# Masks on ScalarE, fixed convolution inputs, and weights split by casting and accumulating transfers in a two-block transformer kernel

## The chip, the cores and the metric

The kernel runs on one core of one Trainium2 chip. The metric is the time of one execution on the device in microseconds. The kernel before took 1448.87 us, the median of three runs (1448.43 to 1448.95).

The engines go by their names in the profile: PE is TensorE (matmuls; PEld is its loading of the stationary operand), DVE is VectorE, ACT is ScalarE, POOL is GpSimd, and SP is the queue that issues most transfers.

## The reference

Two different blocks act one after the other on 512 tokens of width 1024, all in float32. Biases, masks and gains are left out here.

```python
# first block
hn = rmsnorm(h, norm_mix_w)
q, k, v, z, xbc, dt_raw = split(hn @ w_in)
att = chunk_band_attention(q, k, v, rel_bias)          # 8 heads of 64
xbc = silu(causal_depthwise_conv(xbc, conv_w, conv_b))  # 4 taps, 1536 channels
y = ssd_scan(x, dt, A, Bm, Cm) + d_skip * x             # 16 heads, 2 groups, state 128
ssd = gated_group_norm(y * silu(z))
h = h + concat([att, ssd]) @ w_out
h = h + square(relu(rmsnorm(h) @ w_ff1)) @ w_ff2        # 4096 hidden
h = rmsnorm(h)
# second block
z = rmsnorm(x) @ w_in_2                                 # pooled part, q, k, v
y_pool = pool_mixer(u_pool);  y_attn = diff_attention(q, k, v)
gates = sigmoid(h @ w_gate + b_gate)
x = x + (gates_0 * (y_pool @ w_branch_pool) + gates_1 * (y_attn @ w_branch_attn)) @ w_out_2
x = x + square(relu(rmsnorm(x) @ w_up)) @ w_down
```

In the scan, the decay between two positions of a chunk is the exponential of a difference of running sums of `dt * A`.

## The kernel before, in words

**Three matmuls for one.** TensorE multiplies in a reduced float32 format (`F32R`). So that the result is accurate, every operand is split into a high part, which is the value rounded to that format, and a low part, which is the value less its high part. A product is then three matmuls: high by high, high by low and low by high (`mm3` and `mm3s`, lines 167 to 175).

**The weight stream.** Most weights lie in device memory as 172 units of 128 x 1024 float32 (512 KB), in the order of use. `load_unit` (L132) brings the next unit to a raw tile `wr` (pool `wraw`, three buffers) by SP's queue. `ahead` (L144) runs at the first use of each unit: it loads up to three units ahead of the use and splits up to two ahead. The split is a ScalarE copy into a tile `wh` (L156, pool `whi`, two buffers) and a subtraction into a tile `wl` (L157, pool `wlo`, two buffers), on VectorE, or on POOL for units 1 and 3 only. Both are marked with high priority. `st["lim"]` holds the splitting back, not the loading.

**Order of the work.** TensorE's instructions keep the order in which the program writes them. `drive` advances one dense product and, between its steps, a step of the side jobs (convolution, scan, attention). For the other engines a planner orders the instructions by priority and by its own estimate of when they are ready; each engine's queue then works strictly in that order. A tile of a pool takes a buffer that has been released by all its readers.

**First stage.** `dense1` (L789) projects the convolution's channels first: four blocks of B and C by `quad`, then eight of x by `rows`. Each block ends in `conv` (L475). It takes an input tile `u` of 515 columns (two buffers), clears its first three columns on POOL (L477), scales the product into the rest (L478), and forms four taps (L480 on ScalarE, L482 on VectorE), a tanh and a product (L485, L486). `xs_side` (L544) then transposes the blocks on TensorE (L548).

**Masks.** `dt_side` makes `da`, split into `dah` and `dal`, for 4 chunks x 16 heads. For the scan, `am_pair` (L560) multiplies a 128 x 128 triangle (`le`) by four of these columns at once, on POOL: 128 x 512 for the high part (L563), and the same for the low part (L565). There are 16 pairs: two for each of four chunks and two groups. A pair is the moving operand of L599 and L600.

**Feed-forward.** It runs in two blocks, `a` and `b`, each in four quarters. A quarter first makes 1024 hidden channels with 8 units of the stream (`hidden`), then `second` (L943) multiplies them by a part of the second matrix, with a scheme of seven products for eight (sums and differences of halves). The second matrix does not pass through the unit stream: `load2` (L888) brings 128 x 1024 tiles `u` and `v`, and `prep` (L910) forms their differences and splits them. A half-width operand goes through `narrow` (L893; tiles `vh` and `vl`). A full-width one goes through `wide` (L898), which takes its tiles **from the pools `whi` and `wlo`** of the unit stream and splits by L298 on ScalarE and L299 on VectorE. `second` walks through stages 0, 1 and 2 with four steps each; stages 0 and 1 have one wide operand in each step, stage 2 none. A step prepares operands up to two steps ahead. The first two are prepared in the hidden stage, ahead of the use of its last unit. In the last step of a stage, the products are done in the reverse order:

```python
            for r, key in enumerate(seq):
                for m in seq[r:r + 3]:
                    prep(m)
                if r == len(seq) - 2:
                    st["lim"] = N_UNITS
                    ahead()
                ...
                for t in (reversed(todo) if e else todo):
                    prod(*t)
```

**Second block.** Its attention (`a2_first` to `a2_third`) keeps POOL in use: squares (L1172), scalings (L1178, L1275), the second map's weight (L1252), and `stack_q`'s low part (L358).

Of the kernel before, what the change touches and what calls it, by code (L numbers as in the profile page):

```python
# [9 lines left out]
F32 = mybir.dt.float32  # L10
F32R = mybir.dt.float32r
I32 = mybir.dt.int32
AF = mybir.ActivationFunctionType
ALU = mybir.AluOpType
# [4 lines left out]
T = 512  # L19
# [6 lines left out]
N_UNITS = 172  # L26
# [22 lines left out]
def bc_mid(ap, n):  # L49
    return ap.rearrange("p (o a) -> p o a", o=1).to_broadcast([ap.shape[0], n, ap.shape[1]])  # L50


def bc_in(ap, n):
    return ap.rearrange("p (a o) -> p a o", o=1).to_broadcast([ap.shape[0], ap.shape[1], n])
# [36 lines left out]
def mixer_kernel(ctx, tc, xT, xN, wst, wfa, wfb, wdt, wgrp, rbt, par, con, frow, out):  # L91
    nc = tc.nc
    V, S, G, PE = nc.vector, nc.scalar, nc.gpsimd, nc.tensor

    const = ctx.enter_context(tc.tile_pool(name="const", bufs=1))
    base = ctx.enter_context(tc.tile_pool(name="base", bufs=1))
    wraw_p = ctx.enter_context(tc.tile_pool(name="wraw", bufs=3))
    whi_p = ctx.enter_context(tc.tile_pool(name="whi", bufs=2))
    wlo_p = ctx.enter_context(tc.tile_pool(name="wlo", bufs=2))
    sm = ctx.enter_context(tc.tile_pool(name="sm", bufs=3))  # L100
    ps_mm = ctx.enter_context(tc.tile_pool(name="ps_mm", bufs=4, space=PSUM))
    ps_ax = ctx.enter_context(tc.tile_pool(name="ps_ax", bufs=4, space=PSUM))
# [16 lines left out]
    def C(name):  # L119
        a, b = _CON[name]  # L120
        return con_sb[:, a:b]
# [2 lines left out]
    wdt_sb = const.tile([128, KD, 16], F32, name="wdt")  # L124

    st = {"raw": {}, "dma": 0, "hl": {}, "split": 0, "use": 0, "pool": 2, "tick": 0, "lim": N_UNITS}
    RAW_AHEAD, SPLIT_AHEAD = 3, 2

    def parts(j):
        return [slice(0, 512), slice(512, 1024)] if j == 0 else [slice(0, 1024)]  # L130

    def load_unit(between=None):  # L132
        j = st["dma"]
        if j < N_UNITS:
            t = wraw_p.tile([128, 1024], F32, tag="wr", name="wr")
            for p in parts(j):
                nc.sync.dma_start(out=t[:, p], in_=wst[j][:, p])
                if between:
                    between()
                    between = None  # L140
            st["raw"][j] = t
            st["dma"] += 1

    def ahead():  # L144
        u = st["use"]
        with tc.high_priority():
            while st["dma"] < min(u + RAW_AHEAD, N_UNITS):
                load_unit()
            while st["split"] < min(u + SPLIT_AHEAD, st["lim"]):
                j = st["split"]  # L150
                t = st["raw"].pop(j)
                hi = whi_p.tile([128, 1024], F32R, tag="wh", name="wh")
                lo = wlo_p.tile([128, 1024], F32R, tag="wl", name="wl")
                eng = G if st["pool"] and j % st["pool"] == 1 else V
                for p in parts(j):
                    S.activation(out=hi[:, p], in_=t[:, p], func=AF.Copy)  # L156
                    eng.tensor_tensor(out=lo[:, p], in0=t[:, p], in1=hi.bitcast(F32)[:, p], op=ALU.subtract)  # L157
                st["hl"][j] = (hi, lo)
                st["split"] += 1

# [16 lines left out]
    def col(w, j):  # L177
        return w[:, j * 128:(j + 1) * 128]
# [122 lines left out]
    def v3(ap, a=NT):  # L301
        return ap.rearrange("p (a b) -> p a b", a=a)
# [100 lines left out]
    with ExitStack() as ph:  # L403
        fa_p = ph.enter_context(tc.tile_pool(name="m1f", bufs=1))
        s_p = ph.enter_context(tc.tile_pool(name="m1s", bufs=2))
        c_p = ph.enter_context(tc.tile_pool(name="m1c", bufs=1))
# [40 lines left out]
        def small(name, n=64):  # L447
            return c_p.tile([128, n], F32, name=name)

        dx, du, dz, dz2, dp, dt, da, dal = (  # L450
            small(n) for n in ("dx", "du", "dz", "dz2", "dp", "dt", "da", "dal"))
        dah = c_p.tile([128, 64], F32R, name="dah")
        aexp = small("aexp", 16)
        ex = small("ex", 192)
        dtdo = small("dtdo")

        xs_tok, conv_out, lw = {}, {}, {}
        ready = set()

# [13 lines left out]
            yield True  # L473

        def conv(f, b):  # L475
            u = s_p.tile([128, T + 3], F32, tag="u", name="u", bufs=2)
            G.memset(u[:, 0:3], 0.0)  # L477
            V.tensor_tensor(out=u[:, 3:], in0=b, in1=lw["rb1"], op=ALU.mult)  # L478
            a = FA.get()
            S.activation(out=a, in_=u[:, 3:], func=AF.Identity, bias=cb_[:, f:f + 1], scale=cw[:, 36 + f:37 + f])  # L480
            for j in range(3):
                V.scalar_tensor_tensor(out=a, in0=u[:, j:j + T], scalar=cw[:, j * 12 + f:j * 12 + f + 1], in1=a,  # L482
                                       op0=ALU.mult, op1=ALU.add)
            t = FA.get()
            S.activation(out=t, in_=a, func=AF.Tanh)  # L485
            V.scalar_tensor_tensor(out=a, in0=t, scalar=1.0, in1=a, op0=ALU.add, op1=ALU.mult)  # L486
            FA.put(t)
            conv_out[f] = a
            ready.add(("conv", f))
# [70 lines left out]
        def am_pair(c, g, q):  # L560
            o = c * 16 + g * 8 + q * 4
            amh, aml = RA.take(2)
            G.tensor_tensor(out=v3(amh), in0=bc_mid(C("le"), 4), in1=bc_in(dah.bitcast(F32)[:, o:o + 4], 128),  # L563
                            op=ALU.mult)
            G.tensor_tensor(out=v3(aml), in0=bc_mid(C("le"), 4), in1=bc_in(dal[:, o:o + 4], 128), op=ALU.mult)  # L565
            return amh, aml

        def ssd_side():
# [472 lines left out]
    with ExitStack() as ph:  # L1041
# [39 lines left out]
        us = {}  # L1081
# [415 lines left out]
```

## Time and profile before

| | |
|---|---|
| median of three runs | 1448.87 us |
| the profiled execution | 1448.68 us |
| its span | 1446.9 us |
| TensorE busy | 1423.2 us (98%) |
| VectorE busy | 1019.4 us (70%) |
| ScalarE busy | 660.8 us (46%) |
| POOL busy | 276.8 us (19%) |
| L157 (low parts of units) | 171 instructions, 231.8 us |
| L156 (high parts of units) | 173 instructions, 182.5 us |
| moved by transfers | 145.90 MB |

A line of a group gives the source line, the engine, the operation, the tile written and the tiles read, the shape and the count; then busy time and the mean of one instruction in ns, and the idle time of that engine just before these instructions, with what ended it. A line of the timeline gives start and length in us; what stands in brackets at its end is idle time before it and what ended it. A line of waits gives the total in us, the number of waits and the longest. A line of a stretch of time gives its length, the busy time of PE, PEld, DVE, ACT and POOL with counts, the granted clock of TensorE as a share, the busy share of the 16 transfer engines, and GB/s. A line of transfers gives what is moved, the issuing queue, the count, the size, and the median us from issue to landing.

### The profile page before, as it was taken

The page shows a single profiled execution, that of the slowest core. Times are in us where ns is not written, and L with a number is a line of the kernel's source. Part 1 is how long each engine was busy: PE and PEld are TensorE (multiplying, and loading weights), DVE is VectorE, ACT ScalarE, POOL GpSimd, SP SyncE. Part 2 cuts the span into 40 slices and gives each one's busy share as a digit, 9 for nine tenths or more (in the row PEclk, how much of TensorE's full clock was granted, in tenths as well). Part 3 has the DMA queues.
Part 4 walks back from the last instruction along what each step waited for, and adds up shares of the span by engine and source line. Part 5 has one row for each costly group of instructions (what it writes and reads, how often), then busy time and mean ns, then how long its engine had stood idle before and what let it go on. Part 6 is the DMA issues. An engine that isn't in the chain of part 4 may idle for free.

```text
span 1446.9 us, 17960 instructions
## 1 busy us (share of the span) xinstructions
PE 1423.2 (98%) x6683; PEld 1172.2 (81%) x6683; DVE 1019.4 (70%) x1761; ACT 660.8 (46%) x1108; POOL 276.8 (19%) x264
## 2 busy tenths in 40 slices
PE   8979999999999999999999999999999999999998
PEld 6857888888888888888878888888888888888887
DVE  7885665655977768677784666777645977878676
ACT  5433445433644435355444646464324544444452
POOL 4664730000010010102262433221110010010101
PEclk9999999999999999999999999999999999999999
DMA  7212532223433241520333433341233433141401
GB/s 255 83 50 65 139 98 82 69 88 116 175 97 114 65 149 44 160 74 30 94 92 95 124 95 100 101 122 62 88 102 133 158 114 105 58 146 45 160 30 58
DMA packets 46407, 145.90 MB, mean 101 GB/s; under 512 B 5872, under 2 KB 6128, under 8 KB 46320
## 3 DMA queue, kind: packets, MB, share of 16 engines
q1 hardware_dynamic: 46320, 144.76, 32.1%
q8 instruction: 52, 0.85, 0.2%
q14 instruction: 35, 0.29, 0.1%
HBM read 131.63 MB, written 2.10 MB: 92 GB/s over the span
## 4 chain that ended last, share of the span: by engine, by line
PE 82%; DVE 9%; POOL 3%; issue 3%; DMA 1%; ACT 1%; SPq 0%; POOLq 0%; DVEq 0%; ACTq 0%
PE mm L168 12%; PE mm L170 12%; PE mm L169 12%; PE mm L173 10%; PE mm L174 10%; PE mm L175 10%; DVE wl L157 2%; PE ax L175 2%; PE ax L173 2%; PE ax L174 2%; DVE s L1253 1%; PE ax L723 1%; PE ax L1265 1%; PE ax L382 1%; PE ax L617 1%
## 5 line engine op out<-in xcount | busy, mean ns | idle before, releaser
L168 PE MATMUL mm<-r,wh 128*128 128x512 f32 x928 | 368.5, 397 | 0.0
L170 PE MATMUL mm<-r,wl 128*128 128x512 f32 x928 | 362.1, 390 | 1.1 <-DVE wl L157 1.1
L169 PE MATMUL mm<-r,wh 128*128 128x512 f32 x928 | 362.0, 390 | 0.9 <-DVE r L294 0.9
L156 ACT ACTIVATE wh<-wr 128x1024 fp32r<-128x1024 f32 (+1 forms) x173 | 182.5, 1055 | 379.4 <-PE mm L169 147.1
L157 DVE TENSOR_TENSOR wl<-wr,wh 128x1024 fp32r<-128x1024 f32 (+1 forms) x171 | 231.8, 1355 | 111.7 <-ACT wh L156 111.1
L173 PE MATMUL mm<-wh,r 128*128 128x512 f32 x512 | 206.0, 402 | 0.0
L169 PEld LDWEIGHTS mm<-r,wh 128*128 128x128 f32 x928 | 174.7, 188 | 38.4 <-issue 1.4
L170 PEld LDWEIGHTS mm<-r,wl 128*128 128x128 f32 x928 | 174.5, 188 | 38.4 <-DVE wl L157 1.5
L168 PEld LDWEIGHTS mm<-r,wh 128*128 128x128 f32 x928 | 174.8, 188 | 37.3 <-issue 1.9
L175 PE MATMUL mm<-wh,r 128*128 128x512 f32 x512 | 200.0, 391 | 0.0
L174 PE MATMUL mm<-wl,r 128*128 128x512 f32 x512 | 199.5, 390 | 0.3 <-DVE wl L157 0.3
L299 POOL TENSOR_TENSOR vl<-u,vh 128x512 fp32r<-128x512 f32 x36 | 47.8, 1330 | 754.9 <-ACT vh L298 754.5
L174 PEld LDWEIGHTS mm<-wl,r 128*128 128x128 f32 x512 | 96.3, 188 | 21.5 <-issue 1.9
L173 PEld LDWEIGHTS mm<-wh,r 128*128 128x128 f32 x512 | 96.2, 188 | 20.8 <-issue 1.9
L175 PEld LDWEIGHTS mm<-wh,r 128*128 128x128 f32 x512 | 96.1, 188 | 20.7
L298 ACT ACTIVATE vh<-u 128x512 fp32r<-128x512 f32 x100 | 63.0, 631 | 53.6 <-PE mm L175 37.5
L933 DVE TENSOR_TENSOR h<-h,mm 128x512 f32<-128x512 f32 x80 | 52.5, 680 | 20.8 <-PE mm L175 20.8
L351 ACT ACTIVATE s<-s,nm 128x128 f32<-128x128 f32 (+1 forms) x96 | 52.7, 550 | 20.9 <-DVE nm L348 20.9
L298 ACT ACTIVATE wh<-u 128x1024 fp32r<-128x1024 f32 (+1 forms) x32 | 32.3, 1008 | 63.0 <-PE mm L175 63.0
L298 ACT ACTIVATE wh<-t 128x1024 fp32r<-128x1024 f32 x32 | 34.0, 1063 | 56.1 <-PE mm L169 32.5
L299 DVE TENSOR_TENSOR wl<-u,wh 128x1024 fp32r<-128x1024 f32 (+1 forms) x32 | 38.0, 1188 | 25.8 <-ACT wh L298 25.8
L299 DVE TENSOR_TENSOR vl<-u,vh 128x512 fp32r<-128x512 f32 x64 | 43.7, 684 | 0.0
(346 smaller groups left out, 2349.4 us busy)
## 6 DMA issues: line engine op xcount, KB each, us to landing
wr<-in_wst_dram SPq DMA_DIRECT2D x171, 512.0 KB, 3.6
u<-in_wfa_dram SPq DMA_DIRECT2D x32, 512.0 KB, 4.5
u<-in_wfb_dram SPq DMA_DIRECT2D x32, 512.0 KB, 4.4
r<-r SPq DMA_DIRECT2D x56, 128.0 KB, 2.9
h<-in_xT_dram SPq DMA_DIRECT2D x8, 256.0 KB, 6.5
h<-in_xN_dram SPq DMA_DIRECT2D x8, 256.0 KB, 5.2
f<-in_rbt_dram SPq DMA_DIRECT2D x8, 256.0 KB, 4.1
gr<-gr SPq DMA_DIRECT2D x16, 128.0 KB, 2.8
```

What stands on the lines that cost most here:

```text
L156: S.activation(out=hi[:, p], in_=t[:, p], func=AF.Copy)
L157: eng.tensor_tensor(out=lo[:, p], in0=t[:, p], in1=hi.bitcast(F32)[:, p], op=ALU.subtract)
L168: PE.matmul(ps, lhsT=wh, rhs=xh, start=first, stop=False)
L169: PE.matmul(ps, lhsT=wh, rhs=xl, start=False, stop=False)
L170: PE.matmul(ps, lhsT=wl, rhs=xh, start=False, stop=last)
L173: PE.matmul(ps, lhsT=xh, rhs=wh, start=first, stop=False, **kw)
L174: PE.matmul(ps, lhsT=xh, rhs=wl, start=False, stop=False, **kw)
L175: PE.matmul(ps, lhsT=xl, rhs=wh, start=False, stop=last, **kw)
L298: S.activation(out=hi, in_=src, func=AF.Copy)
L299: (eng or V).tensor_tensor(out=lo, in0=src, in1=hi.bitcast(F32), op=ALU.subtract)
L351: S.activation(out=s[:, SOFF[i]:SOFF[i] + n], in_=s[:, SOFF[i]:SOFF[i] + n], func=AF.Exp, bias=nm[:, i:i + 1], accum_out=Z[:, i:i + 1])
L933: V.tensor_tensor(out=ht(c, g), in0=ht(c, g), in1=b, op=ALU.add)
```

## The change

- The masks of `am_pair` are made on ScalarE, by four copies of 128 x 128 each, scaled by a column, in place of one POOL instruction of 128 x 512.
- The convolution's inputs `u` are two fixed tiles whose first three columns are cleared once, on VectorE.
- From unit 3 on, a unit is loaded by a transfer that POOL issues and that casts float32 to the reduced format, straight into a tile `wh`. For the low part, ScalarE writes the negated high part into `wl`, and a second transfer issued by POOL adds the unit from device memory to it.
- Units 0 to 2 are loaded and split as before, all on ScalarE and VectorE, with one raw buffer.
- `whi` and `wlo` have four buffers each; loading runs up to four units ahead of the use and splitting three.
- POOL's memory for transfer descriptors is set to 4096 bytes.

```diff
-    wraw_p = ctx.enter_context(tc.tile_pool(name="wraw", bufs=3))
-    whi_p = ctx.enter_context(tc.tile_pool(name="whi", bufs=2))
-    wlo_p = ctx.enter_context(tc.tile_pool(name="wlo", bufs=2))
+    wraw_p = ctx.enter_context(tc.tile_pool(name="wraw", bufs=1))
+    whi_p = ctx.enter_context(tc.tile_pool(name="whi", bufs=4))
+    wlo_p = ctx.enter_context(tc.tile_pool(name="wlo", bufs=4))
...
-    RAW_AHEAD, SPLIT_AHEAD = 3, 2
+    RAW_AHEAD, SPLIT_AHEAD = 4, 3
...
+    RAW_UNITS = 3
+
     def load_unit(between=None):
         j = st["dma"]
-        if j < N_UNITS:
+        if j >= RAW_UNITS and j < N_UNITS:
+            hi = whi_p.tile([128, 1024], F32R, tag="wh", name="wh")
+            G.dma_start(out=hi, in_=wst[j])
+            st["raw"][j] = hi
+            st["dma"] += 1
+        elif j < N_UNITS:
             t = wraw_p.tile([128, 1024], F32, tag="wr", name="wr")
...
                 t = st["raw"].pop(j)
+                lo = wlo_p.tile([128, 1024], F32R, tag="wl", name="wl")
+                if j >= RAW_UNITS:
+                    hi = t
+                    S.activation(out=lo, in_=hi.bitcast(F32), func=AF.Copy, scale=-1.0)
+                    G.dma_start(out=lo, in_=wst[j], accum_op=ALU.add)
+                    st["hl"][j] = (hi, lo)
+                    st["split"] += 1
+                    continue
                 hi = whi_p.tile([128, 1024], F32R, tag="wh", name="wh")
-                lo = wlo_p.tile([128, 1024], F32R, tag="wl", name="wl")
-                eng = G if st["pool"] and j % st["pool"] == 1 else V
                 for p in parts(j):
                     S.activation(out=hi[:, p], in_=t[:, p], func=AF.Copy)
-                    eng.tensor_tensor(out=lo[:, p], in0=t[:, p], in1=hi.bitcast(F32)[:, p], op=ALU.subtract)
+                    V.tensor_tensor(out=lo[:, p], in0=t[:, p], in1=hi.bitcast(F32)[:, p], op=ALU.subtract)
...
+        us = [c_p.tile([128, T + 3], F32, name=f"u{n}") for n in range(2)]
+        for u in us:
+            V.memset(u[:, 0:3], 0.0)
...
         def conv(f, b):
-            u = s_p.tile([128, T + 3], F32, tag="u", name="u", bufs=2)
-            G.memset(u[:, 0:3], 0.0)
+            u = us[f % 2]
...
             amh, aml = RA.take(2)
-            G.tensor_tensor(out=v3(amh), in0=bc_mid(C("le"), 4), in1=bc_in(dah.bitcast(F32)[:, o:o + 4], 128),
-                            op=ALU.mult)
-            G.tensor_tensor(out=v3(aml), in0=bc_mid(C("le"), 4), in1=bc_in(dal[:, o:o + 4], 128), op=ALU.mult)
+            for t, a in ((amh, dah.bitcast(F32)), (aml, dal)):
+                for j in range(4):
+                    S.activation(out=col(t, j), in_=C("le"), func=AF.Copy, scale=a[:, o + j:o + j + 1])
             return amh, aml
...
-    nc = _bacc.Bacc("TRN2", target_bir_lowering=False, num_devices=1)
+    nc = _bacc.Bacc("TRN2", target_bir_lowering=False, num_devices=1, dynamic_dma_scratch_size=4096)
```

## The prediction

> **What bounds the kernel now.** I read the page's busy shares first, then what TensorE waited for, then the two places below in order of time. The page:
>
> ```profile
> span 1446.9 us, 17960 instructions
> ...
> PE 1423.2 (98%) x6683; PEld 1172.2 (81%) x6683; DVE 1019.4 (70%) x1761; ACT 660.8 (46%) x1108; POOL 276.8 (19%) x264
> ```
>
> TensorE is busy for all but 23.7 us of the span. Nothing can be won beyond its waits and the slow matmuls around them, while anything that makes TensorE wait is paid in full. Its waits, longest first:
>
> ```profile
> PE ax L548 <- DVE f L486: 8.6, 1, 8.6
> PE ax L382 <- DVE mx L343: 2.1, 3, 1.1
> PE ax L617 <- DVE f L604: 1.9, 3, 1.3
> ...
> PE mm L170 <- DVE wl L157: 1.1, 1, 1.1
> PE ax L392 <- DVE s L1253: 1.0, 2, 0.6
> ```
>
> One is large. The weights' low part (L157), which the change takes from VectorE, kept TensorE waiting once, for 1.1 us. The large wait in order of time, on POOL, then DVE, then PE:
>
> ```profile
> 61.89 8.90 POOL L563 TENSOR_TENSOR r<-con,dah 128x512 fp32r<-128x512 f32 x6
> 70.75 6.04 POOL L565 TENSOR_TENSOR r<-con,dal 128x512 fp32r<-128x512 f32 x6
> ...
> 77.72 0.10 POOL L477 MEMSET u<- 128x3 f32 x1
> ```
>
> ```profile
> 77.86 2.96 DVE L482 SCALAR_TENSOR_TENSOR f<-u,cw,f 128x512 f32<-128x512 f32 x2 [7.97 <-POOL u L477]
> 80.74 2.06 DVE L157 TENSOR_TENSOR wl<-wr,wh 128x1024 fp32r<-128x1024 f32 x1
> ...
> 85.30 0.68 DVE L486 SCALAR_TENSOR_TENSOR f<-f,f 128x512 f32<-128x512 f32 x1
> ```
>
> ```profile
> 76.91 0.49 PE L548 MATMUL ax<-con,f 128*128 128x128 f32 x3
> 86.04 1.33 PE L548 MATMUL ax<-con,f 128*128 128x128 f32 x5 [8.64 <-DVE f L486]
> ```
>
> The 0.10 us memset of the convolution's input stood on POOL behind a queue of masks; VectorE waited 7.97 us for it, and TensorE 8.64.
>
> The second place is a feed-forward quarter, on ScalarE:
>
> ```profile
> 476.64 1.06 ACT L298 ACTIVATE wh<-t 128x1024 fp32r<-128x1024 f32 x1 [0.66 <-PE mm L169]
> ...
> 482.08 1.06 ACT L298 ACTIVATE wh<-t 128x1024 fp32r<-128x1024 f32 x1 [3.40 <-PE mm L169]
> ...
> 486.39 1.06 ACT L298 ACTIVATE wh<-t 128x1024 fp32r<-128x1024 f32 x1 [1.56 <-PE mm L175]
> ...
> 490.47 1.06 ACT L298 ACTIVATE wh<-t 128x1024 fp32r<-128x1024 f32 x1 [1.38 <-PE mm L175]
> ...
> 509.88 1.06 ACT L156 ACTIVATE wh<-wr 128x1024 fp32r<-128x1024 f32 x1 [2.14 <-PE mm L175]
> ```
>
> Every copy into a wh buffer starts when TensorE frees one. The last two units of the hidden stage are 5.4 us apart (476.64 to 482.08), which is a unit's 24 matmuls with nothing between; the steps of the second product take 4.1. The next unit's copy (509.88) comes after the last wide one: buffers are given in the order of the program, although that unit's copy is marked urgent.
>
> **The change part by part.**
>
> *Masks and convolution inputs.* No memset is left in the path, and POOL loses both groups of masks:
>
> ```profile
> L563 POOL TENSOR_TENSOR r<-con,dah 128x512 fp32r<-128x512 f32 x16 | 22.0, 1389 | 3.4 <-PE ax L599 2.3 <-DMA r<-r 1.1
> L351 ACT ACTIVATE s<-s,nm 128x128 f32<-128x128 f32 x24 | 9.5, 397 | 20.9 <-DVE nm L348 20.9
> L595 ACT ACTIVATE bt<-ax 128x128 f32<-128x128 f32 x6 | 1.6, 268 | 3.1 <-DVE cbm L590 3.1
> ```
>
> Two masks of each kind are 16 x 2 x 4 = 128 copies of 128x128 on ScalarE. By the two rows one takes 268 to 397 ns: 34 to 51 us in all, in eight groups of 16 (4.3 to 6.4 us). The convolution that ended at 85.98 loses the 7.97 us wait, the 2.06 us of L157, and half of the 2.96 us, which were stretched beside POOL: it would end at 74.5, or with a whole group of masks ahead of it on ScalarE at 80.9. The transposes want it at about 77.2. I take the wait as gone (0 to 3.7 us stay). Slow work behind it goes too:
>
> ```profile
> 82.00:89.00 7.00, 2.96 (x10) 2.59 (x11) 7.00 (x11) 4.00 (x6) 1.97 (x3) 0.51 0.23 75
> ```
>
> At a granted clock of 0.51, these 2.96 us held 1.5 us of work. Term: -10 us (-6 to -10).
>
> *Weights in the ordinary stages.* From the fourth unit on, ScalarE's copy becomes a negation of the same size, and VectorE's subtraction a transfer that adds:
>
> ```profile
> L157 DVE TENSOR_TENSOR wl<-wr,wh 128x1024 fp32r<-128x1024 f32 x169 | 230.4, 1363 | 108.1 <-ACT wh L156 107.5
> ...
> L156 ACT ACTIVATE wh<-wr 128x1024 fp32r<-128x1024 f32 x171 | 181.2, 1060 | 377.1 <-PE mm L169 147.1 <-PE mm L175 117.2 <-issue 75.6
> ```
>
> ```profile
> 1300.00:1400.00 100.00, 100.00 (x441) 82.21 (x440) 74.59 (x111) 47.09 (x67) 5.26 (x4) 1.00 0.26 86
> ```
>
> ```profile
> wr<-in_wst_dram SPq DMA_DIRECT2D x171, 512.0 KB, 3.6
> ```
>
> Most of the 230 us leaves VectorE, but it lay beside a busy TensorE: it is worth a part of the small waits on VectorE (L382, L617 and L392, 5.0 us together). I take -1.5 us (0 to -5).
>
> No casting or accumulating transfer, and no transfer issued by POOL, stands in the trace. A plain 512 KB lands after 3.6 us and, by 86 GB/s at a share of 0.26, fills the 16 engines for 1.6 us. The cast I put at one plain transfer; the accumulation, which has to read its target too, between one and four, and take two: 3.2 us of engines, about 5.2 us to landing. An issue costs POOL between 0.1 us (the memset) and 1.5 us (a mask); I take 1. A buffer freed by unit j-4 then holds unit j after 1 + 3.6 + 1.1 + 1 + 5.2 = 11.9 us, while three units of at least 5.4 us, 16.2 in all, stand ahead of it. Hidden: term 0; the cover ends where the chain passes 16.2 us.
>
> POOL works in order. Behind a transfer that waits for TensorE to free a buffer, or for ScalarE's negation, stand POOL's steps of the second attention (L1172, L1178, L1252, L1275) and L358, and TensorE's transposes and scores behind those. One wait of 1.4 us, a mask's length, in each of eight heads would be +11 us; I take 0.
>
> The Trainium skill ("SBUF — State Buffer", "Who interferes with whom") speaks against the change: POOL cannot write transfer descriptors while a VectorE copy in a two-port mode holds the shared port, though a VectorE step with two SBUF inputs blocks POOL's reads only. The masks fit its second half: 1.48 us each in the row from 61.89, most of it beside VectorE, and 1.01 in the next, while VectorE stood still. By it an issue is late by one copy, which the 4.3 us of cover would take; most of VectorE's work here has two inputs.
>
> *The start.* One raw buffer for units 0 to 2 in place of three puts unit 1's load behind unit 0's subtraction:
>
> ```profile
> 6.60 0.69 DVE L157 TENSOR_TENSOR wl<-wr,wh 128x512 fp32r<-128x512 f32 x1 [0.20 <-ACT wh L156]
> ```
>
> From 7.3 us, 3.6 + 1.1 + 1.2 gives 13.2 for unit 1 and 19.1 for unit 2. TensorE begins unit 0 at about 6 and wants them at 12 and 17, so it would be 2 us late; it lost 1.1 on L157 as it is. I take +2 us (-1 to +6, with slower landings).
>
> *Buffers in the second product of the feed-forward.* Here I expect the time. `wide` takes its tiles from the pool of the units' high parts. Today both buffers serve it, since unsplit units wait as raw tiles elsewhere. After the change the units are loaded straight into that pool, four at a time: the next three hidden units sit in three of the four buffers before the third wide is asked for, and leave only in the next hidden stage. From the third wide on, one buffer is left, and each wide waits for the one before it. On DVE and PE:
>
> ```profile
> 488.34 1.22 DVE L299 TENSOR_TENSOR wl<-t,wh 128x1024 fp32r<-128x1024 f32 x1
> ...
> 491.88 1.22 DVE L299 TENSOR_TENSOR wl<-t,wh 128x1024 fp32r<-128x1024 f32 x1
> ```
>
> ```profile
> 490.27 0.39 PE L173 MATMUL ax<-vh,r 128*128 128x512 f32 x1
> ...
> 491.64 0.39 PE L173 MATMUL mm<-wh,afr 128*128 128x512 f32 x1
> 491.87 0.40 PE L174 MATMUL mm<-wl,afr 128*128 128x512 f32 x1
> ```
>
> Let a step start at s. The copy runs from s+0.2 (490.47 after 490.27) to s+1.26, the subtraction to s+2.5, and the low part is usable at about s+2.55. The third step has 1.37 us of narrow matmuls ahead (490.27 to 491.64) and wants the low part at s+1.60: 0.95 lost. The fourth runs reversed and wants it at s+0.23: 2.32. The first three of the next stage want it at s+0.23 too, but get the buffer 1.37 us earlier: 0.96 each. The last, reversed with narrow ones ahead, loses nothing. That is 0.95 + 2.32 + 3 x 0.96 = 6.15 us a quarter. Six quarters lose it in full, one has a half-width second stage (3.3), and the last has no units left to hold (0): 40 us. VectorE also comes late (1.95 and 1.41 us after the copies' starts, where 1.06 would do), up to 1.9 a quarter: 52 us. I take 46.
>
> The Trainium skill ("TensorE: Matmul & The Clock Gate", "What's actually happening") has the clock halved after about 3.4 us without work; by it these waits, 2.3 us at most, cost no more than themselves. The trace shows 0.51 only after the 8.64 us wait; were each of seven quarters slowed once like that, 1.5 us each, 10 us would be added.
>
> **Sum.** The profiled run took 1448.7 us (span 1446.9, and 1.8 around it; the median of the three is 1448.9). 1448.7 - 10 - 1.5 + 0 + 2 + 46 = 1485 us.
>
> **Rivals.** *Covered, faster:* the held units come in after the wides, or two buffers stay free, and TensorE never waits: 1485 - 46 = 1439. It decides from two free buffers on. For it: today's second product runs without a gap on two. Against it: the 509.88 row follows program order, and the loads of three units stand before the third wide there.
>
> *Weights late:* the accumulation fills the engines for more than 3.8 us (5.4 less 1.6 for the cast), 2.4 plain transfers, or lands after more than 9.5. At four plain ones (6.4 us) a unit takes 8.0 us instead of 5.4. Some 45 units of the hidden and gate stages have no other work between and no prefetch left: 45 x 2.6 = 115, so 1600 us. For it: the target must be read and written. Against it: a share of 0.26 leaves room.
>
> *Cancelled:* waits of a quarter of that size (12 us) beside the gains: 1451 less the start, 1449. *Not as said:* masks on ScalarE hold the convolution up as POOL did: 1495.
>
> **How the numbers follow.** Forecast 0.58 (1465 to 1515), weights late 0.22, covered 0.12, cancelled 0.04, not as said 0.04. The range runs from the covered case, 1438, to 1600, with half of the late case above it. Faster by over 0.2% (what a measurement of this kernel can tell from no change) 0.12, within it 0.04, slower 0.84.
>
> **What would show it.** Right: no L548 wait near 77 us; new waits of mm L174 on DVE wl L299, some 35 of 1 to 2.4 us, in seven of the eight second products. Weights late: waits of L168 to L175 on transfers into wl. Wrong: second products without gaps, or POOL issues of several us each.

## The result, and the profile after

The changed kernel takes 1664.26 us (median of four runs, 1663.38 to 1669.34); the kernel before, on the same chip, 1448.82. The ratio is 1.149, 95% interval 1.148 to 1.151. It is slower, as forecast, but by 215 us where 36 were forecast, and it lies above the range of 1438 to 1600. The page of the profiled run:

```profile
span 1661.6 us, 18260 instructions
...
PE 1497.5 (90%) x6683; PEld 1200.5 (72%) x6683; DVE 830.7 (50%) x1596; ACT 694.0 (42%) x1236; POOL 451.4 (27%) x556
...
q0 software_dynamic: 48672, 177.23, 47.3%
...
L163 POOL DMA_DIRECT2D wl<-in_wst_dram x169 | 149.4, 890 | 680.7 <-ACT wl L162 612.2
...
L138 POOL DMA_DIRECT2D wh<-in_wst_dram x169 | 124.7, 763 | 208.4 <-PE mm L188 117.3
...
wh<-in_wst_dram POOLq DMA_DIRECT2D x169, 512.0 KB, 6.3
wl<-in_wst_dram POOLq DMA_DIRECT2D x169, 512.0 KB, 5.7
```

The same 6683 matmuls now keep TensorE busy for 74 us more (1497.5 against 1423.2), and TensorE is idle for 164 us of the span instead of 24. So two thirds of the loss are waits, and one third is matmuls that take longer. What TensorE waits for, and after it what all engines wait for longest, with total, number and longest:

```profile
PE mm L183 <- DMA wl<-in_wst_dram: 42.5, 23, 3.7
PE ax L405 <- DVE s L1269: 14.0, 18, 1.8
PE ax L187 <- DVE wl L312: 13.7, 18, 0.8
PE mm L187 <- DVE wl L312: 12.9, 15, 2.3
```

```profile
POOL wl L163 <- ACT wl L162: 612.2, 119, 13.0
ACT wl L162 <- DMA wh<-in_wst_dram: 394.3, 102, 9.0
```

(L181 to L183 and L186 to L188 are the matmuls that were L168 to L170 and L173 to L175; L138 is the casting load, L162 the negation, L163 the adding transfer, L312 the wide tiles' subtraction, L1268 and L1269 the second attention's L1252 and L1253.) The 8.64 us wait of L548 on the convolution is not among TensorE's waits any more. In its place the weights' low parts are late, and on POOL and ScalarE stand the two waits by which one instruction at the head of a queue holds up all behind it.

Where the time went, by stage. TensorE works its matmuls in the same order in all kernels here, so a stage is timed from one matmul to the same matmul in each trace. Times in us; the eight hidden stages and the eight second products of the feed-forward are taken together, and "other" is the rest. The second attention's column starts with the second block's first matmul and ends at about the fourth of its eight heads; "other" holds the row products, the gate, the two output products, and the attention steps beside them:

| kernel | first units | conv., scan | hidden x8 | second x8 | attention 2 | other |
|---|---|---|---|---|---|---|
| before | 35.7 | 141.3 | 353.6 | 311.8 | 230.6 | 369.0 |
| after | 44.9 | 149.9 | 422.5 | 369.2 | 272.2 | 398.0 |
| masks and inputs alone | 36.3 | 140.1 | 353.6 | 311.8 | 230.7 | 369.0 |
| after, two buffers held free | 44.7 | 152.6 | 390.3 | 315.8 | 263.6 | 403.4 |
| after, load ahead of the addition | 44.8 | 138.8 | 363.2 | 373.7 | 249.2 | 373.8 |
| after, five buffers | 45.6 | 140.0 | 364.9 | 359.6 | 237.5 | 367.9 |
| after, no addition | 45.6 | 135.9 | 359.6 | 363.6 | 236.3 | 367.9 |
| after, order and no addition | 44.8 | 137.4 | 353.7 | 369.3 | 231.2 | 370.9 |
| five buffers, two free | 45.9 | 140.0 | 365.9 | 311.2 | 233.2 | 367.8 |
| ordered, two free, three raw | 38.4 | 138.4 | 365.6 | 321.1 | 238.9 | 367.9 |

The second products lost 57 us, as large as the forecast's largest term, but the hidden stages lost 69, the second attention 42 and the others 29, where the forecast had nothing.

**The loop.** A hidden stage of the changed kernel, on POOL and on ScalarE:

```profile
481.23 0.90 POOL L138 DMA_DIRECT2D wh<-in_wst_dram  x1
...
495.65 0.87 POOL L163 DMA_DIRECT2D wl<-in_wst_dram  x1 [12.20 <-ACT wl L162]
496.26 0.84 POOL L138 DMA_DIRECT2D wh<-in_wst_dram  x1
503.82 0.85 POOL L163 DMA_DIRECT2D wl<-in_wst_dram  x1 [6.73 <-ACT wl L162]
504.37 1.44 POOL L138 DMA_DIRECT2D wh<-in_wst_dram  x2
```

```profile
502.47 1.06 ACT L162 ACTIVATE wl<-wh 128x1024 fp32r<-128x1024 f32 x1 [5.92 <-DMA wh<-in_wst_dram]
...
510.65 1.06 ACT L162 ACTIVATE wl<-wh 128x1024 fp32r<-128x1024 f32 x1 [4.08 <-DMA wh<-in_wst_dram]
```

Read the two together. The load of one unit is issued at 496.26 and has landed at about 502.4, when the negation starts (502.47). POOL stands at the addition (L163) until the negation is done, issues it at 503.82, and only then, at 504.37, issues the next load (two of them, since a second buffer has come free by then). This turn takes 504.37 - 496.26 = 8.1 us: 6.2 for the landing, 1.35 to the addition's issue, 0.55 to the next load's. TensorE needs a unit every 5.4 us. TensorE had left the buffer for the next load at about 495.7 (two units of 5.4 us from the stage's start at 484.8); nothing but POOL's order held it back. The turn before was longer still, 15.0 us from load to load: the load of 481.23 landed only at about 494.1, as three additions and six 512 KB tiles of the second matrix were under way and the transfer engines were full (share 1.04 to 1.06 from 480 to 492). The turn after it took 10.4 us for its two loads. For two of the stage's eight units the low part came too late, and TensorE waited 2.12 and 2.45 us. Its rows at these waits, and behind the second the granted clock of the stretch (0.50) with that of the next:

```profile
509.33 0.50 PE L183 MATMUL mm<-r,wl 128*128 128x512 f32 x1 [2.12 <-DMA wl<-in_wst_dram]
...
514.70 0.39 PE L182 MATMUL mm<-r,wh 128*128 128x512 f32 x1
517.53 0.50 PE L183 MATMUL mm<-r,wl 128*128 128x512 f32 x1 [2.45 <-DMA wl<-in_wst_dram]
...
519.22 0.63 PE L183 MATMUL mm<-r,wl 128*128 128x512 f32 x1
```

```profile
518.80:522.20 3.40, 3.40 (x9) 2.63 (x8) 0.00 (x0) 0.69 (x1) 0.00 (x0) 0.50 1.05 353
522.20:525.60 3.40, 3.40 (x16) 2.82 (x15) 1.54 (x3) 1.71 (x4) 1.42 (x2) 1.00 0.31 39
```

**The second product.** TensorE's waits in one of them:

```profile
549.86 0.49 PE L186 MATMUL mm<-wh,afr 128*128 128x512 f32 x1 [1.15 <-ACT wh L311]
551.12 0.50 PE L187 MATMUL mm<-wl,afr 128*128 128x512 f32 x1 [0.77 <-DVE wl L312]
556.36 0.50 PE L187 MATMUL ax<-wl,r 128*128 128x512 f32 x1 [0.77 <-DVE wl L312]
...
566.83 0.50 PE L187 MATMUL ax<-wl,r 128*128 128x512 f32 x1 [0.76 <-DVE wl L312]
```

From 551.12 on the steps are 5.24 us apart (551.12 to 566.83 is three), where the steps of before took 4.1: each wide waits for the one before it to leave the single buffer that is left. Six of the eight products took 45.4 to 46.1 us instead of 38.7; the last of the first block, after which the second attention starts, 56.7 instead of 41.1; the very last, with no units left to hold, 39.3.

### The profile page after: what moved, and what is told of

It is laid out like the page before. It is cut to its first block, busy times and chain, and to the rows that moved or that the text cites. A ratio compares the mean times of both kernels' runs of the same rounds, so it can differ in the third digit from the quotient of the medians.

```text
span 1661.6 us, 18260 instructions
## 1 busy us (share of the span) xinstructions
PE 1497.5 (90%) x6683; PEld 1200.5 (72%) x6683; DVE 830.7 (50%) x1596; ACT 694.0 (42%) x1236; POOL 451.4 (27%) x556
## 4 chain that ended last, share of the span: by engine, by line
PE 31%; issue 24%; DMA 19%; POOL 10%; DVE 8%; ACT 7%; SPq 0%; POOLq 0%; ACTq 0%; DVEq 0%
DMA wh<-in_wst_dram 12%; PE mm L183 5%; PE mm L181 4%; PE mm L182 4%; PE mm L187 4%; DMA wl<-in_wst_dram 4%; PE mm L188 3%; POOL wl L163 3%; PE mm L186 3%; DVE wl L312 3%; POOL wh L138 2%; ACT wh L311 2%; ACT wl L162 2%; PE ax L187 1%; DMA r<-r 1%
## 5 line engine op out<-in xcount | busy, mean ns | idle before, releaser
L183 PE MATMUL mm<-r,wl 128*128 128x512 f32 x928 | 375.5, 405 | 46.8 <-DMA wl<-in_wst_dram 42.5
L181 PE MATMUL mm<-r,wh 128*128 128x512 f32 x928 | 380.0, 410 | 14.7 <-ACT g L1168 8.8
L182 PE MATMUL mm<-r,wh 128*128 128x512 f32 x928 | 372.8, 402 | 10.7 <-DVE r L307 10.5
L162 ACT ACTIVATE wl<-wh 128x1024 fp32r<-128x1024 f32 x169 | 176.8, 1056 | 471.4 <-DMA wh<-in_wst_dram 394.3
L163 POOL DMA_DIRECT2D wl<-in_wst_dram x169 | 149.4, 890 | 680.7 <-ACT wl L162 612.2
L183 PEld LDWEIGHTS mm<-r,wl 128*128 128x128 f32 x928 | 180.8, 195 | 96.4 <-DMA wl<-in_wst_dram 52.8
L186 PE MATMUL mm<-wh,r 128*128 128x512 f32 x512 | 210.3, 411 | 15.0 <-ACT g L1180 5.9
L181 PEld LDWEIGHTS mm<-r,wh 128*128 128x128 f32 x928 | 181.5, 196 | 56.1 <-ACT g L1168 9.0
L182 PEld LDWEIGHTS mm<-r,wh 128*128 128x128 f32 x928 | 181.2, 195 | 51.6 <-DVE r L307 11.3
L187 PE MATMUL mm<-wl,r 128*128 128x512 f32 x512 | 204.2, 399 | 6.7 <-DMA wl<-in_wst_dram 6.7
L188 PE MATMUL mm<-wh,r 128*128 128x512 f32 x512 | 203.6, 398 | 0.0
L138 POOL DMA_DIRECT2D wh<-in_wst_dram x169 | 124.7, 763 | 208.4 <-PE mm L188 117.3
L186 PEld LDWEIGHTS mm<-wh,r 128*128 128x128 f32 x512 | 98.4, 192 | 39.3 <-ACT g L1180 7.0
L187 PEld LDWEIGHTS mm<-wl,r 128*128 128x128 f32 x512 | 98.3, 192 | 30.2 <-DMA wl<-in_wst_dram 9.0
L188 PEld LDWEIGHTS mm<-wh,r 128*128 128x128 f32 x512 | 98.5, 192 | 21.4
L312 POOL TENSOR_TENSOR vl<-u,vh 128x512 fp32r<-128x512 f32 x36 | 51.1, 1512 | 228.3 <-ACT vh L311 165.3
L312 DVE TENSOR_TENSOR wl<-u,wh 128x1024 fp32r<-128x1024 f32 (+1 forms) x32 | 37.0, 1157 | 70.7 <-ACT wh L311 70.7
L312 DVE TENSOR_TENSOR wl<-t,wh 128x1024 fp32r<-128x1024 f32 x32 | 39.2, 1224 | 36.5 <-ACT wh L311 36.5
```

The lines of the kernel that those rows point to most:

```text
L138: G.dma_start(out=hi, in_=wst[j])
L162: S.activation(out=lo, in_=hi.bitcast(F32), func=AF.Copy, scale=-1.0)
L163: G.dma_start(out=lo, in_=wst[j], accum_op=ALU.add)
L181: PE.matmul(ps, lhsT=wh, rhs=xh, start=first, stop=False)
L182: PE.matmul(ps, lhsT=wh, rhs=xl, start=False, stop=False)
L183: PE.matmul(ps, lhsT=wl, rhs=xh, start=False, stop=last)
```

## The experiments

**Masks and inputs alone**, on the kernel before:

```
-            u = s_p.tile([128, T + 3], F32, tag="u", name="u", bufs=2)
-            G.memset(u[:, 0:3], 0.0)
+            u = us[f % 2]
...
+            for t, a in ((amh, dah.bitcast(F32)), (aml, dal)):
+                for j in range(4):
+                    S.activation(out=col(t, j), in_=C("le"), func=AF.Copy, scale=a[:, o + j:o + j + 1])
```

> The kernel before with the masks on ScalarE and the fixed convolution inputs alone; weights as before. The prediction's term: the 8.64 us wait of TensorE on the convolution is gone, 1449 - 10 = 1439 us (ratio 0.993). Rival: in the changed kernel the stage of convolutions and scan became 8.6 us longer although that wait is gone; if the 128 mask copies on ScalarE are the reason, and not the weights, the time is 1449 to 1458 us.

1447.72 us, ratio 0.9991 (0.9982 to 1.0000): hardly anything, between the prediction's term (1439) and the rival's range, and close to the rival's lower end. The wait of L548 is gone, but ScalarE now reads as follows, and then TensorE:

```profile
62.20 2.16 ACT L568 ACTIVATE r<-con,dah 128x128 fp32r<-128x128 f32 x7 [4.89 <-POOL dah L530]
...
65.44 0.39 ACT L568 ACTIVATE r<-con,dah 128x128 fp32r<-128x128 f32 x1
...
67.42 1.26 ACT L568 ACTIVATE r<-con,dah 128x128 fp32r<-128x128 f32 x4
68.59 1.04 ACT L156 ACTIVATE wh<-wr 128x1024 fp32r<-128x1024 f32 x1
```

```profile
69.68 0.50 PE L168 MATMUL mm<-r,wh 128*128 128x512 f32 x1 [2.90 <-ACT wh L156]
...
70.94 0.50 PE L170 MATMUL mm<-r,wl 128*128 128x512 f32 x1 [0.53 <-DVE wl L157]
...
71.63 0.63 PE L169 MATMUL mm<-r,wh 128*128 128x512 f32 x1
```

A mask on ScalarE takes 0.39 us by itself and starts 0.29 us after the one before it in a row; twenty of them, with one other step (a tanh), fill 62.20 to 68.59. Behind them stands the next unit's copy into wh, for which TensorE waits 2.90 us and runs slowly for a while. Matmul for matmul against before, the kernel falls 5.6 us behind there, wins 9.6 at the convolution that used to be late, and loses part of it again a little later.

**The inputs alone** (the first half of that diff; masks stay on POOL):

> The kernel before with the two fixed convolution inputs alone; masks stay on POOL, weights as before. With the masks on ScalarE and these inputs the 8.64 us wait was gone, but the weights' copies into wh stood behind the masks on ScalarE (2.90 us wait and slow work behind it), and 1.3 us were won. If the removed memset alone frees the convolution: 1449 - 8 to 10 = 1439 to 1441 us. Rival (the transposes then wait for the masks or the scan on POOL, a step later): 1445 to 1449 us.

1448.00 us, ratio 0.9994 (0.9985 to 1.0003): no change that can be measured; the rival's range held, but not its mechanism. TensorE's longest wait, then POOL, then VectorE ahead of the masks and beside them:

```profile
PE mm L173 <- DVE u L481: 6.3, 1, 6.3
```

```profile
63.24 8.81 POOL L566 TENSOR_TENSOR r<-con,dah 128x512 fp32r<-128x512 f32 x6
72.01 9.26 POOL L568 TENSOR_TENSOR r<-con,dal 128x512 fp32r<-128x512 f32 x6
```

```profile
59.63 0.74 DVE L485 SCALAR_TENSOR_TENSOR f<-u,cw,f 128x512 f32<-128x512 f32 x1
...
72.52 4.42 DVE L485 SCALAR_TENSOR_TENSOR f<-u,cw,f 128x512 f32<-128x512 f32 x3
```

The removed memset lets VectorE start, but beside POOL's masks, from 63.24 on, each of its steps takes 1.47 us (4.42 for three) instead of 0.74, and TensorE waits 6.3 us for VectorE to empty a product's bank (L481). This agrees with the Trainium skill ("SBUF — State Buffer", "Who interferes with whom"), by which a VectorE instruction with two SBUF inputs contends with a POOL instruction that reads SBUF.

**Two buffers held free for wide**, on the changed kernel:

```
-            while st["dma"] < min(u + RAW_AHEAD, N_UNITS):
+            while st["dma"] < min(u + RAW_AHEAD, N_UNITS, st["lim"] + 2):
```

> The changed kernel, but while the second product of the feed-forward runs at most two units of the next hidden stage are loaded, so that two of the four high-part buffers are left for wide. Theory of held buffers: each second product goes from 45.4 back to 38.7 us, seven of them, 47 us less: about 1617 us. Rival (the low part's subtraction on VectorE is late by itself, whatever the buffers): second products stay at 45 us and the time at 1664 us, or rises by up to 10 us, since the next hidden stage starts with fewer units at hand.

1577.38 us, ratio 1.088: 87 us less, 53 of them in the second products (315.8 us of 311.8 in the kernel before) and 32 in the hidden stages, which the expectation did not have. The expectation was 47 us less. The held units are shown as the cause of the second products' loss. Why the hidden stages gain with them was not tried apart: POOL's instructions also come in another order in this kernel.

**The load ahead of the addition.** The program's own order is load of unit j+1, then addition of unit j; the planner had turned most of these pairs round (109 of 168). The edit lays the program's order down:

```
+            his[j] = G.dma_start(out=hi, in_=wst[j])
...
+                    with tc.issue_after(his[j + 1].ins) if j + 1 in his else ExitStack():
                         G.dma_start(out=lo, in_=wst[j], accum_op=ALU.add)
```

> The changed kernel with one order laid down on POOL: the casting load of unit j+1 is issued ahead of the accumulating transfer of unit j. Theory of the blocked queue: in the changed kernel POOL stands at the accumulation of unit j until the negation is done, and issues the next load only then, so that loads run one after the other, one unit per 8.1 us; with the order laid down the loads come a unit earlier, the 394 us that ScalarE's negations wait for loads fall below 200, the hidden stages go from 50 to 44 to 46 us and the time falls by 60 to 120 us, to 1545 to 1605. Rival (the transfers themselves are too slow, or the 16 engines too full): the waits stay and the time is within 15 us of 1664.

1550.69 us, ratio 1.070: 114 us less, as the theory of the blocked queue had it (the negations' wait for loads, though, is 245 us and not below 200). The load that opens the stage still lands late (issued at 455.38, negation at 464.99), but now TensorE does not wait for it. The same stage as above on POOL, the loads now 5.4 us apart and ahead of the additions, each waiting for TensorE alone (L139 is the load, L165 the addition):

```profile
470.59 0.56 POOL L139 DMA_DIRECT2D wh<-in_wst_dram  x1 [3.40 <-PE mm L185]
471.13 0.90 POOL L165 DMA_DIRECT2D wl<-in_wst_dram  x1
476.03 0.55 POOL L139 DMA_DIRECT2D wh<-in_wst_dram  x1 [4.00 <-PE mm L185]
477.17 0.85 POOL L165 DMA_DIRECT2D wl<-in_wst_dram  x1 [0.58 <-ACT wl L163]
```

The second hidden stage whole, by a window each (length, busy time of PE, PEld, DVE, ACT, POOL, granted clock, share of the DMA engines, GB/s), first of the changed kernel, then with the order laid down:

```profile
484.80:535.20 50.40, 45.83 (x194) 37.10 (x194) 27.27 (x49) 18.96 (x29) 7.72 (x11) 0.97 0.64 167
```

```profile
459.50:503.00 43.50, 43.50 (x194) 36.03 (x193) 25.71 (x46) 18.93 (x29) 7.67 (x11) 1.00 0.79 183
```

With the same transfers TensorE is busy without a gap for 43.50 us, which is what the kernel before takes. The engines are fuller than in the slow version (0.79 against 0.64): by themselves they were not the limit.

**Five high-part buffers, three low-part ones, loads five ahead:**

```
-    whi_p = ctx.enter_context(tc.tile_pool(name="whi", bufs=4))
-    wlo_p = ctx.enter_context(tc.tile_pool(name="wlo", bufs=4))
+    whi_p = ctx.enter_context(tc.tile_pool(name="whi", bufs=5))
+    wlo_p = ctx.enter_context(tc.tile_pool(name="wlo", bufs=3))
...
-    RAW_AHEAD, SPLIT_AHEAD = 4, 3
+    RAW_AHEAD, SPLIT_AHEAD = 5, 3
```

> The changed kernel with five buffers for the high parts and three for the low parts, and loads started five units ahead instead of four; splits still three ahead. Theory of the blocked queue: a load is issued a unit (5.4 us) earlier, has landed before its negation is due, and neither ScalarE nor POOL stands at the head of its queue for it: 1530 to 1600 us, with the seven slow second products still in it (one free buffer as before). Rival of slow transfers: with 3.2 us of landing time beyond what a unit has, more lead moves only the first units of a stage, and the time stays within 20 us of 1664.

1517.93 us, ratio 1.047: 146 us less, and 12 below the expected range. In this kernel all loads stand on POOL ahead of the addition of the unit before, so it opens the loop by the order too, and not by the lead alone. ScalarE's negations wait for TensorE now (177 us on L183, to free a low-part buffer) and no longer for loads; the second products keep their loss, as expected.

**No addition.** The second transfer overwrites the low part, so that this kernel leaves the addition out; the order on POOL is that of the changed kernel:

```
-                    G.dma_start(out=lo, in_=wst[j], accum_op=ALU.add)
+                    G.dma_start(out=lo, in_=wst[j].bitcast(F32R))
```

> The changed kernel with the second transfer overwriting the low part instead of adding to it (this leaves the addition out of the computation; all instructions, their order on every queue and the bytes read stay). Rival of slow transfers (the addition, which must read its target, is what TensorE waits for): landing falls from 5.7 us towards 4, and the time falls by more than 60 us below 1664. Theory of the blocked queue: POOL still stands at each second transfer until the negation is done, and the time stays within 40 us of 1664.

1515.31 us, ratio 1.046: 149 us less. Here the theory of the blocked queue, as it stood, fell: it had said no more than 40.

The queues and landings of its page, and POOL in a hidden stage:

```profile
q0 software_dynamic: 48672, 177.23, 38.6%
...
wh<-in_wst_dram POOLq DMA_DIRECT2D x169, 512.0 KB, 4.6
wl<-in_wst_dram POOLq DMA_DIRECT2D x169, 512.0 KB, 4.0
```

```profile
460.80 0.53 POOL L138 DMA_DIRECT2D wh<-in_wst_dram  x1 [0.18 <-PE mm L183]
466.58 0.53 POOL L163 DMA_DIRECT2D wl<-in_wst_dram  x1 [5.25 <-ACT wl L162]
467.10 0.54 POOL L138 DMA_DIRECT2D wh<-in_wst_dram  x1
```

The other transfer, the load that was not touched, lands in 4.6 us instead of 6.3. In the changed kernel the load of 496.26 is issued 0.6 us behind an addition (495.65) and shares the engines with it. Without the addition's longer work the same turn is 6.3 us (460.80 to 467.10) instead of 8.1. That is still over 5.4, but it does not go on: the next load, at 471.68, has waited 4.03 us for TensorE, and the stage takes 43.5 us. What the addition costs the engines can be estimated from the shares: with it 0.473 x 1661.6 / 338 = 2.33 us for a mean transfer of POOL, without it 0.386 x 1514.0 / 338 = 1.73; if the casts cost the same in both, an addition takes 2 x 2.33 - 1.73 = 2.9 us of all 16 engines, where a cast takes 1.7.

**Both** edits, the order and no addition, to tell two costs from two ways into one loop:

> The changed kernel with both: the order laid down on POOL, and the second transfer overwriting instead of adding (this leaves the addition out). Order alone gave -114 us, no addition alone -149 us. If they are two ways into one loop (load, negation, second issue, next load: 8.1 us a unit where 5.4 are there), either breaks it, and together they give little more than the better one: 1495 to 1515 us, the rest being the seven second products (48 us) and the start (10 us). Rival (two separate costs that add up): 1664 - 114 - 149 = 1401, or at least below 1480.

1514.76 us, ratio 1.046, the same as without the addition alone. The two do not add up. The loss needs both: an order that issues a load only after the addition before it, and an addition that makes that load land late. Take away either and a unit is ready in time, in the hidden stages to within 10 us of 353.6 together. They are not quite even: with the order laid down the addition still costs 36 us (1550.69 against 1514.76), half of it in the second attention, while with the addition left out the order is worth nothing.

**Five buffers and two of them free**, on the five-buffer kernel:

```
+            while st["dma"] < min(u + RAW_AHEAD, N_UNITS, st["lim"] + 3):
```

> The kernel with five high-part buffers and, during the second product, at most three units of the next hidden stage in them, so that two are left for wide. If held buffers and blocked queue are separate and add up: 1518 - 48 (seven second products from about 45.5 back to 38.7) = 1470 us. Rival (with two free buffers the next hidden stage is short of units): second products 38.7, but hidden stages 2 us or more longer each, and 1485 us or more.

1468.18 us, ratio 1.013: 50 us less, as the theory had it, so the held units and the blocked queue are separate costs. All second products are back (311.2 us). What is left over before, 19 us, is in the first units (10) and the first hidden stage of each block (6 each).

**Two raw buffers for the first three units**, on that kernel, and **three raw buffers**, on the kernel with the order laid down, with `st["lim"] + 2` as the limit on loads and three low-part buffers:

```
-    wraw_p = ctx.enter_context(tc.tile_pool(name="wraw", bufs=1))
+    wraw_p = ctx.enter_context(tc.tile_pool(name="wraw", bufs=2))
```

> The previous kernel (five high-part buffers, two of them left for wide) with two raw buffers for the first three units instead of one. Theory: the 9 to 10 us that the first units lose are the third unit's load behind the single raw buffer: 8 to 10 us less than the previous kernel, about 1461 us. Rival (the start is late because POOL's first casting load waits, or because loads into h take the engines): less than 3 us of gain.

> The kernel with the laid-down order on POOL (four high-part buffers), two of them left for wide during the second product, and three raw buffers for the first three units as before the change (low parts in three buffers). From 1551: - 48 for the second products = 1503. Theory A of the start (a second raw buffer gained nothing, since the third unit's load still stood behind other loads on SP's queue; with three it goes out at once, as before the change): first units 36 to 38 us instead of 45, total about 1494 us. Theory B (the third unit's subtraction is behind other work on VectorE, which has all three of them now, whatever the raw buffers): first units stay at 44 us or more, total 1500 to 1506.

With two, 1468.32 us, no gain where 8 to 10 us were expected. With three, 1475.98 us, where theory A had about 1494: the first units take 38.4 us instead of 44.8, near theory A's 36 to 38, and the free buffers gave 53 us in the second products and 10 in the second attention, where 48 were expected. One buffer holds the third unit's load back, and by then SP's queue is full of other loads. In the changed kernel, on SP, and then on ScalarE and TensorE:

```profile
11.33 11.36 SPq L483 DMA_DIRECT2D h<-in_xN_dram  x7
23.46 0.33 SPq L144 DMA_DIRECT2D wr<-in_wst_dram  x1
```

```profile
27.83 1.06 ACT L169 ACTIVATE wh<-wr 128x1024 fp32r<-128x1024 f32 x1 [10.00 <-DMA wr<-in_wst_dram]
```

```profile
17.88 0.80 PE L181 MATMUL mm<-r,wh 128*128 128x512 f32 x1 [3.67 <-ACT wh L169]
23.49 0.80 PE L183 MATMUL mm<-r,wl 128*128 128x512 f32 x1 [4.38 <-DVE wl L170]
```

The third unit's load goes out at 23.46 behind seven loads of h. With two buffers it went out at 12.57, but the unit's subtraction still stood behind others on VectorE's queue until 25.64. So theory A holds for the kernel with three, and theory B names what was left in the kernel with two.

**More lead for the masks**, on the kernel with masks and inputs alone: three high and three low buffers (the room is taken from POOL's transfer scratch, as in the change) and splits three ahead and loads four; then the same with the fourth unit's subtraction on VectorE:

```
-    RAW_AHEAD, SPLIT_AHEAD = 3, 2
+    RAW_AHEAD, SPLIT_AHEAD = 4, 3
...
-                eng = G if st["pool"] and j % st["pool"] == 1 else V
+                eng = G if st["pool"] and j % st["pool"] == 1 and j != 3 else V
```

> The kernel before with the masks on ScalarE and the fixed convolution inputs, and three buffers instead of two for the high and the low parts, with splits three units ahead instead of two (weights otherwise as before). If the 1.3 us that the masks and inputs gain without it are the 9.6 us at the convolution less 5.6 us of weights' copies behind the masks on ScalarE and later small losses, then one unit (5.4 us) more of lead covers the 2.90 us wait: 1441 to 1444 us. Rival (the next wait, on the scan or on VectorE, takes the gain again): 1446 to 1449 us.

> The kernel before with the masks on ScalarE, the fixed convolution inputs and three buffers for high and low parts (as in the run with more lead), and the fourth unit's subtraction on VectorE instead of POOL. With more lead the convolutions and scan took 138.1 us instead of 141.3 and the later stages 1.6 us less, but the first units 42.1 instead of 35.7: on POOL that subtraction stood ahead of two of the sums for the norm, and TensorE waited 4.7 us for them. If this queue order is the whole loss at the start: 1448.5 - 6.4 + 1.6 = about 1443 us (ratio 0.996), faster than both kernels. Rival (VectorE's norm steps are late instead): 1446 to 1449 us.

1448.46 us, ratio 1.0001 (0.9993 to 1.0010), and 1445.98 us, ratio 0.9979 (0.9970 to 0.9988). With the lead, convolutions and scan take 138.1 us, 3.2 less than before; in the first of the two kernels the start gives it back (42.1 us against 35.7), so that its time falls into the rival's range; in the second most of that is mended (38.0), and it ends between the expected 1443 and the rival's 1446. The second beats both kernels by a little more than a measurement can tell from nothing. What holds it at the start is still POOL's sums for the norm:

```profile
PE ax L275 <- POOL f L269: 2.3, 1, 2.3
```

## Why the prediction was wrong, point by point

**Weights in the ordinary stages, term 0: this step failed, and it is most of the miss.** The forecast followed one buffer and added up its chain, 11.9 us, against a cover of 16.2. The pieces of the chain hold: additions land after 5.7 us (5.2 taken), take 2.9 us of the engines (3.2 taken), and an issue costs POOL 0.76 to 0.89 us (1 taken). Only the load's landing was well off, 6.3 in the median instead of 3.6 (and 12.9 for the load that opens the stage above). With the medians the chain is still about 15 us, inside the cover. What failed is that three such chains were taken to run side by side. The text said itself that POOL works in order, and priced that for the second attention, but did not ask what stands behind an addition on POOL: the next unit's load. With that the chains run one after the other, in a turn of 8.1 us against 5.4 for a unit. The experiment with the order laid down shows it (114 us less), and the one without the addition shows the other half of the condition. (TensorE's waits on L157 in the kernel before were two, 1.1 and 0.3 us, and not one; the sum does not hang on it.)

**Weights late, the rival at 1600 us with a chance of 0.22**, forecast the waits that came (L183 on transfers into wl), but by a condition that did not hold: additions over 3.8 us of engines or landing after 9.5. A chance built on the transfers' speed alone was too low; there was a second way to the same waits.

**POOL's in-order wait in the second attention, priced at 11 us, taken as 0:** that stage lost 42 us in the trace. Laying the order down gives back 23 of them, leaving the addition out as well 41; with five buffers the loss is 7 and with two of them free 2.6. So the loop and the additions' work are its causes in the main. The wait that was priced is in the trace too: TensorE waits 14.0 us, in 18 waits, on L1269, which takes what POOL's L1268 makes (1.0 us in two waits before, on L1253), though partly behind the end of this stage; with the order laid down it is 4.8. What single transfers on POOL did to it was not tried apart.

**The second product, term 46: right.** The trace shows 57 us, 9 of them beyond a usual quarter in the one ahead of the second attention; leaving two buffers free gave 50 us on the five-buffer kernel, when nothing else was in the way. Place, partner (L187 on L312) and the exempt last quarter are as forecast. The 33 waits of L187 are near the forecast 35, but 18 of them, 13.7 us together, are of at most 0.8 us. A usual quarter lost 6.7 us where the buffer's chain alone gave 6.15, so there is little left for VectorE's part. The quarter ahead of the second attention was to lose half as much (3.3) and lost 15.6; why was not looked into.

**Masks and inputs, term -10: the wait is gone, the gain is 1.3 us.** The forecast asked whether masks on ScalarE delay the convolution; it did not ask what else ScalarE does there. The next unit's copy stands behind twenty masks. The price of a mask (0.27 to 0.40 us forecast, 0.39 measured) was right. With the inputs alone there was no gain either; there VectorE's steps took twice as long beside POOL's masks, and TensorE waited for them. The term of -1.5 for small waits is of the size of what the gate's stage shows without the loop (other: -1.2 us); a finer reading is not to be had.

**The start, term +2 (up to +6): 9.2 us.** The chain from 7.3 us on left out SP's queue: the load that has to wait for the raw buffer loses its place and stands behind seven loads of h.

**Slow matmuls, term 0.** The forecast went by the Trainium skill ("TensorE: Matmul & The Clock Gate", "What's actually happening"), which has the clock halved after an idle window of about 3.4 us, and took waits below that as free of it. Here the granted clock is 0.50 for 3.4 us after a wait of 2.45, so the trace does not agree with that reading of it; after the 2.12 us wait in the same stage it stayed at 1.00. By this, a half-speed stretch of 3.4 us costs about 1.7, an estimate. That 74 us of TensorE's time are longer matmuls is read from the page's busy times. Of these the clock accounts for 59 at most, by its mean over the span (0.963 against 0.998 before): 0.037 x 1661.6 - 0.002 x 1446.9. What the rest is was not shown.

## What to carry to other kernels

Where two instructions of a repeated chain share an in-order queue and the second waits for a result, ask what is issued behind it: a chain that fits its cover for one buffer can still run one turn after the other, and the period of that loop, not the length of the chain, is to be set against the work. The order that counts is the planner's and not the program's, so lay it down where a loop closes through it. A step taken off one busy engine lands in another engine's queue ahead of something, and the price is what that something holds up.

## What was not expected of the hardware

By the estimate above, a casting load of 512 KB issued by POOL took 1.7 us of the 16 engines, about what a plain one took in the kernel before (1.6), but an adding one 2.9. With adding transfers on the same queue a load landed after 6.3 us in the median, and after 4.6 when these only overwrote. Issuing from POOL took 0.76 and 0.89 us for load and addition in the changed kernel, and 0.55 for both when nothing was added. And TensorE's clock fell to half after a wait of 2.45 us, for 3.4 us.
